# One memory ring for activations and token operands, the residual added later, weights first at the change of halves

## The chip, the core and the metric

The kernel runs on one core of one Trainium2 chip. The metric is the device time of one launch in microseconds (us). Three timed runs of the kernel before took 2837.26, 2839.12 and 2840.42 us. The core has engines that run side by side, each working through its own instructions in order: TensorE (PE) multiplies matrices, VectorE (DVE), ScalarE (ACT) and GpSimd (POOL) do elementwise work, SyncE (SP) issues DMAs. SBUF is the memory on the core, PSUM the eight banks into which PE accumulates. A tile is a piece of one of these memories. A ring is a set of equal tiles that are handed out in turn, and whoever wants one waits until the last user of it is done.

## The reference

One decoder layer on 2048 tokens of width 1024 in float32. What follows the attention, and matters here, is (`mix` is the gated sum of two attention branches):

```
x  = x + mix @ w_out                                   # out-projection, residual
h2 = rmsnorm(x, ln2_g)                                 # second norm
x  = x + square(relu(h2 @ w_up)) @ w_down              # w_up 1024 x 4096, w_down 4096 x 1024
```

## The kernel before

Every float32 product is made of three matmuls: each operand is split into a high part (a CAST on ACT) and a low part (a subtraction on POOL or DVE), `split` at L90, and `mm3` (L94) issues high x low, low x high and high x high (L96 to L98). A "128x512 matmul" below is one of the three.

The stages follow each other: in-projection and attention (to about 850 us of the span), gates and branches (to 1345), out-projection with the second norms (to 1553), up-projection (to about 2190), down-projection (2219 to 2833).

**Out-projection.** For each block of 128 tokens, PE multiplies, DVE adds the residual, and x goes out to `x2_dram`. `norm2_pre` (L776) squares the row on ACT into an own tile `junk`, POOL makes the scale (`ssy`, `rsxy` in `rms_scale`, L121), and DVE scales into `hn`. `norm2_post` (L783) transposes on PE and writes `hb`. For each pair of blocks POOL makes four differences (`hsum`, L809, names T1 to T4, a ring of three tiles), and each is stored to DRAM (`b_dram`).

**Up-projection.** The two matrix products of the MLP use the seven-product scheme of Strassen and Winograd, so the operands are sums: B11, T1, T2, B22, T3, B21, T4 of the tokens, and A11, S1, S2, S4, S3, A12, A22 of the weights. The tokens come in two halves (hf 0 and 1) of 1024. In each half `token_operand` (L831) loads and splits the seven token operands once, two loads of 512 KB each (`rb`), and 16 steps f follow. A step f loads two weight blocks (`rwu`, 512 KB each), `up_operands` (L848) makes its seven operands, and `up_products` (L919) runs seven products of 12 matmuls into three PSUM banks pa, pb, pc. ACT and DVE turn these into seven activation operands, which lie in one tile `u` of 7 x 512 (ring of two, plus three single tiles), and one DMA of 1792 KB stores them (L954). The weights of half 1, f = 0 are loaded after the last step of half 0 (the call of `up_operands` behind `up_products`, L1022).

**Down-projection.** Before it starts, the pools of the up-projection are released (L1028) and a pool `poolV` takes their place. `acc`, eight tiles that hold the result, is filled from `x2_dram` by 16 loads of 512 KB (L1037). Eight steps F follow, in each four groups g of tokens, in each seven products i. For each, `u_operand` (L1043) loads 256 KB of an activation operand (`ru`, on SP), splits it into `uo` (ACT, then POOL; a ring of nine), PE runs 24 matmuls into banks `pd`, and DVE adds them to `acc` (L1072). The weights (`rwd`) of the next F are loaded and split by `next_down_operands` (L998) after g = 1: seven operands wB11, wT1 and so on.

The raw loads of every stage share a ring `raw` of three tiles of 512 KB. All DMAs are issued by SP. A scheduler that simulates the program sets the order of the instructions on each engine. The order on chip is then fixed, and an instruction that waits holds up those behind it on its engine.

## Time and profile before

| | |
|---|---|
| median of three runs | 2839.12 us |
| profiled execution | 2838.56 us |
| its span (first to last instruction) | 2836.8 us |
| PE busy | 2729.4 us, 96% |
| POOL busy | 1581.9 us, 56% |
| DVE busy | 1510.3 us, 53% |
| ACT busy | 1285.9 us, 45% |
| DMA | 121 GB/s on average |

The profile is of one execution, whose time is 1.76 us longer than its span. PE is the engine to look at, because it is busy nearly throughout: time can only be won where it waits or runs slowly. PEclk in the views is the clock that was granted to TensorE, as a share of full speed, and DMA is the mean busy share of 16 DMA engines.

### The profile page before, as it was taken

What the parts mean: (1) busy time and instruction counts of PE and PEld (TensorE: products, weight loads), DVE (VectorE), ACT (ScalarE), POOL (GpSimd) and SP (SyncE); (2) the same over time, 40 slices, a digit from 0 to 9 for tenths busy, and PEclk for the clock granted to TensorE, in tenths of its full rate; (3) what the DMA queues carried; (4) which work ended last, traced back from release to release, by engine and by line L of the source; (5) the groups of instructions that cost most, each with busy time, mean ns of one, the idle gap of its engine ahead of it and who ended that gap; (6) DMA issues with size and microseconds to landing.
All of it is one profiled execution on the core that took longest, in us unless ns stands there. A gap on an engine that the chain in (4) does not pass through costs nothing.

```text
span 2836.8 us, 38641 instructions
## 1 busy us (share of the span) xinstructions
PE 2729.4 (96%) x13897; PEld 2280.2 (80%) x13897; DVE 1510.3 (53%) x2816; ACT 1285.9 (45%) x2607; POOL 1581.9 (56%) x1375
## 2 busy tenths in 40 slices
PE   8999999999979999999998999979999699999999
PEld 7888888887867888888787788868887588888887
DVE  7776665668995214111444443444344566666654
ACT  5565665667885213111222555555555333333331
POOL 6566666676671111111245766766675777777763
PEclk9999999999999999999999999999999899999999
DMA  5321010011234324222577455565546744444335
GB/s 170 98 71 52 11 57 12 15 57 37 58 102 151 93 68 152 84 63 68 194 225 230 153 155 163 163 186 164 157 151 204 260 128 127 125 123 121 106 108 175
DMA packets 372593, 342.83 MB, mean 121 GB/s; under 512 B 18080, under 2 KB 305840, under 8 KB 372400
## 3 DMA queue, kind: packets, MB, share of 16 engines
q1 hardware_dynamic: 372400, 340.36, 39.5%
q8 instruction: 109, 1.79, 0.3%
q14 instruction: 84, 0.69, 0.1%
HBM read 220.57 MB, written 119.73 MB: 120 GB/s over the span
## 4 chain that ended last, share of the span: by engine, by line
PE 85%; DMA 4%; POOL 4%; DVE 4%; issue 2%; ACT 1%; SPq 1%; POOLq 0%; DVEq 0%; ACTq 0%
PE pd L96 7%; PE pd L98 7%; PE pd L97 7%; PE pg L98 4%; PE pg L96 4%; PE pg L97 4%; PE psA L96 4%; PE psA L98 4%; PE psA L97 4%; PE pa L96 3%; PE pa L98 3%; PE pa L97 3%; PE pb L96 3%; PE pb L98 3%; PE pb L97 3%; PE sp L416 2%
## 5 line engine op out<-in xcount | busy, mean ns | idle before, releaser
L1072 DVE TENSOR_TENSOR acc<-acc,pd 128x512 f32<-128x512 f32 x448 | 298.3, 684 | 212.2 <-PE pd L98 212.1
L92 POOL TENSOR_TENSOR uo<-ru,uo 128x512 fp32r<-128x512 f32 x224 | 305.7, 1374 | 158.8 <-ACT uo L91 155.9
L91 ACT CAST uo<-ru 128x512 fp32r<-128x512 f32 x224 | 138.2, 621 | 344.8 <-PE pd L98 209.5
L96 PE MATMUL psA<-wah,hsh 128*128 128x512 f32 x512 | 208.6, 407 | 2.5 <-ACT hsh L91 1.0
L97 PE MATMUL psA<-wal,hsh 128*128 128x512 f32 x512 | 201.9, 394 | 5.2 <-DVE wal L92 5.2
L98 PE MATMUL psA<-wah,hsl 128*128 128x512 f32 x512 | 201.4, 393 | 1.2 <-DVE hsl L92 1.2
L97 PE MATMUL pd<-wT,uo 128*128 128x512 f32 x512 | 199.7, 390 | 0.0
L96 PE MATMUL pd<-wT,uo 128*128 128x512 f32 x512 | 198.4, 391 | 1.1 <-ACT wT L91 1.1
L98 PE MATMUL pd<-wT,uo 128*128 128x512 f32 x512 | 196.8, 389 | 0.0
L96 PE MATMUL pd<-wB,uo 128*128 128x512 f32 x384 | 150.2, 391 | 23.6 <-ACT uo L91 23.4
L97 PE MATMUL pd<-wB,uo 128*128 128x512 f32 x384 | 149.9, 390 | 0.0
L98 PE MATMUL pd<-wB,uo 128*128 128x512 f32 x384 | 148.7, 389 | 0.0
L653 DVE TENSOR_TENSOR sig<-sig,pb 128x512 f32<-128x512 f32 x64 | 43.7, 685 | 191.2 <-PE pb L98 169.5
L97 PE MATMUL psB<-wal,hsh 128*128 128x256 f32 x512 | 144.9, 283 | 0.0
L98 PE MATMUL psB<-wah,hsl 128*128 128x256 f32 x512 | 144.8, 283 | 0.0
L92 POOL TENSOR_TENSOR hsl<-hT,hsh 128x512 fp32r<-128x512 f32 x80 | 119.6, 1496 | 45.0 <-ACT hsh L91 40.6
L96 PE MATMUL psB<-wah,hsh 128*128 128x256 f32 x512 | 143.7, 281 | 0.0
L312 DVE TENSOR_REDUCE hss<-sq 128x8 f32<-128x512 f32 x64 | 43.8, 685 | 181.6 <-ACT sq L311 181.5
L318 POOL TENSOR_TENSOR hrs<-hss,mhalf 128x8 f32<-128x8 f32 (+1 forms) x64 | 137.2, 2143 | 5.2
L92 POOL TENSOR_TENSOR wg_1l<-rg,wg_1h 128x1024 fp32r<-128x1024 f32 x16 | 42.1, 2631 | 165.0 <-ACT wg_1h L91 130.6
L91 ACT CAST hsh<-hT 128x512 fp32r<-128x512 f32 x128 | 109.8, 858 | 47.3 <-PE psB L97 42.3
L345 POOL TENSOR_TENSOR qn<-qn,gains 128x512 f32<-128x512 f32 x48 | 69.8, 1455 | 81.0 <-DVE qn L342 72.9
(546 smaller groups left out, 8223.0 us busy)
## 6 DMA issues: line engine op xcount, KB each, us to landing
u_dram<-u SPq DMA_DIRECT2D x32, 1792.0 KB, 7.5
ru<-u_dram SPq DMA_DIRECT2D x224, 256.0 KB, 2.7
rwu<-in_w_up_dram SPq DMA_DIRECT2D x64, 512.0 KB, 3.8
x<-in_x_dram SPq DMA_DIRECT2D x32, 512.0 KB, 4.0
rg<-in_w_in_dram SPq DMA_DIRECT2D x32, 512.0 KB, 3.7
rwd<-in_w_down_dram SPq DMA_DIRECT2D x64, 256.0 KB, 3.1
rw<-in_w_in_dram SPq DMA_DIRECT2D x28, 384.0 KB, 3.4
hT_dram<-hT SPq DMA_DIRECT2D x16, 512.0 KB, 3.9
```

The costliest lines, as they stand in the source:

```text
L91: nc.scalar.copy(hi, src)
L92: (eng or nc.vector).tensor_tensor(lo, src, hi, op=ALU.subtract)
L96: nc.tensor.matmul(out, lhs[0], rhs[0], start=first, stop=False, skip_group_check=more)
L97: nc.tensor.matmul(out, lhs[0], rhs[1], start=False, stop=False, skip_group_check=more)
L98: nc.tensor.matmul(out, lhs[1], rhs[0], start=False, stop=last, skip_group_check=more)
L312: nc.vector.tensor_reduce(ss[:, 0:8], sq, axis=AX, op=ALU.add)
L318: nc.gpsimd.tensor_tensor(rs[:, 0:nh], ss[:, 0:nh], mhalf[:, 0:nh], op=ALU.pow)
L345: nc.gpsimd.tensor_tensor(q4, q4, gains[:, 0:2, :].unsqueeze(2).broadcast_to([P, 2, 4, HD]), op=ALU.mult)
L416: nc.tensor.matmul(sp[:, e * 256:e * 256 + nk], ring[:, own, q_, :], ring[:, slots, k_, :], start=(i == 0), stop=(i == 1))
L653: nc.vector.tensor_tensor(gate[m, c, a], gate[m, c, a], pb, op=ALU.mult)
L1072: nc.vector.tensor_tensor(t, t, p, op=ALU.add)
```

## The change

Seven edits: (1) The activations, the single tiles and the token operands of the down-projection share one ring of 18 tiles of 128x512 in `poolU`, which is no longer released between the stages. The store per step f becomes seven stores of 256 KB. (2) `u_load` loads two activation operands at a time (512 KB), and all but the first three of these 128 loads are issued by ACT. (3) `acc` is no longer loaded. In F = 0 the first product to touch each piece is copied by ACT, and the residual is loaded in 32 pieces of 256 KB during F = 1 and 2 and added by POOL. (4) `next_down_operands` is called after g = 2. (5) In the last step of half 0 the weight operands of half 1 are called for ahead of the products. (6) In the last step of half 1 the first three activation loads and four splits are called for ahead of the products. (7) In the out-projection `junk` is gone (the square goes into `hn`, now a ring of three), `hsum` is a ring of two, the low parts of the first four token operands are all made by DVE, and two sums of the weights of f = 0 (S4, S3) move from DVE to POOL.

```diff
-        junk = O4(f"junky{i}", "junk", 1, BF16)
-        rs = rms_scale(xt, junk, poolO, i, "y")
-        hn[i] = O4(f"hn{i}", "hn", 2, F32)
+        hn[i] = O4(f"hn{i}", "hn", 3, F32)
+        rs = rms_scale(xt, hn[i], poolO, i, "y")
...
-            t = poolO.tile([P, 4, P], F32, tag="hsum", bufs=3, name=f"hsum{n}_{i}")
+        return poolO.tile([P, 4, P], F32, tag="hsum", bufs=2, name=f"hsum{n}_{i}")
...
-            split(t[0][:, ks, :], t[1][:, ks, :], rv, nc.gpsimd if q else nc.vector)
+            split(t[0][:, ks, :], t[1][:, ks, :], rv, nc.gpsimd if q and (hf, o) > (0, 3) else nc.vector)
...
-        put("S4", summed("4", a12, s2, ALU.subtract, nc.vector))
-        put("S3", summed("3", a11, a21, ALU.subtract, nc.vector))
+        eng = nc.vector if f else nc.gpsimd
+        put("S4", summed("4", a12, s2, ALU.subtract, eng))
+        put("S3", summed("3", a11, a21, ALU.subtract, eng))
...
-    def Ft(name):
-        return poolF.tile([P, 512], F32, tag="f", bufs=3, name=name)
+    def Ft(name, dtype=F32):
+        return poolU.tile([P, 512], dtype, tag="u", bufs=18, name=name)
...
-        nc.sync.dma_start(u_ops_dram[hf][f // 2][:, :, :, f % 2, :], u.rearrange("p o (j t) -> p o j t", j=4))
+        for o in (6, 1, 0, 2, 4, 5, 3):
+            nc.sync.dma_start(u_ops_dram[hf][f // 2][:, o, :, f % 2, :], u[o].rearrange("p (j t) -> p j t", j=4))
...
+    def u_load(F, g, o):
+        hf, j = g // 2, 2 * (g % 2)
+        no = min(2, 7 - o)
+        r = raw(f"ru{F}_{g}_{o}").rearrange("p (o n) -> p o n", o=2)
+        queue = nc.sync if (F, g) == (0, 0) and o < 6 else nc.scalar
+        queue.dma_start(r[:, 0:no].rearrange("p o (j f t) -> p o j f t", j=2, f=2),
+                        u_ops_dram[hf][F][:, o:o + no, j:j + 2, :, :])
...
+        t = [Ft(f"uo{e}{F}_{g}_{o}", F32R) for e in "hl"]
+        split(t[0], t[1], u_raw.pop((F, g, o)), nc.gpsimd)
...
+            if last and hf == 0:
+                A_next = up_operands(1, 0)
+            if last and hf == 1:
+                for o in (0, 2, 4):
+                    u_load(0, 0, o)
+                U_first = [u_operand(0, 0, o) for o in range(4)]
             up_products(hf, f, A, Bops[hf], then)
-            if f + 1 < NF or hf == 0:
-                A_next = up_operands(hf + last, 0 if last else f + 1)
+            if not last:
+                A_next = up_operands(hf, f + 1)
...
-    poolF.release()
-    poolU.release()
-    poolV = tc.alloc_tile_pool(name="mV", bufs=1, reuse_waits="tile")
...
-            nc.sync.dma_start(a[:, c, :], x2_dram[i * P:(i + 1) * P, :])
...
+    def add_residual(p, c, n):
+        ns = slice(n * 512, (n + 1) * 512)
+        r = poolS.tile([P, 512], F32, tag="S", bufs=12, name=f"rx2_{p}_{c}_{n}")
+        nc.sync.dma_start(r, x2_dram[acc_block(p, c), ns])
+        nc.gpsimd.tensor_tensor(acc[p][:, c, ns], acc[p][:, c, ns], r, op=ALU.add)
...
-                U = u_operand(F, g, i)
+                U = U_first.pop(0) if U_first else u_operand(F, g, i)
+                if 1 <= F <= 2 and i in (3, 6):
+                    for n in range(2):
+                        add_residual(2 * ((g + 3) % 4) + i // 6, (F - 1) % 2, n)
...
-                    nc.vector.tensor_tensor(t, t, p, op=ALU.add)
+                    if F == 0 and i in (0, 1, 2, 6):
+                        nc.scalar.copy(t, p)
+                    else:
+                        nc.vector.tensor_tensor(t, t, p, op=ALU.add)
...
-            if g == 1 and F + 1 < NFF:
+            if g == 2 and F + 1 < NFF:
                 next_down_operands(F + 1, B_NAMES)
```

SP's queue at the change of halves, before. `rwu0_15` are the weights of half 0, step 15, `rb1_T2` to `rb1_T4` token operands of half 1, `rwu1_0` the first weights of half 1, `u_0_13` to `u_0_15` the activations of the last steps:

```order
L853 DMA rwu0_15_1_17671<-in_w_up_dram 128x4x256
L841 DMA rb1_T2_0_17729<-b_dram1_T2_13820 128x1024
L954 DMA u2_dram0_6_15429<-u_0_13_17403 3584x1x128
L841 DMA rb1_T2_1_17733<-b_dram1_T2_13820 128x1024
L841 DMA rb1_B22_0_17752<-b_dram1_B22_13821 128x1024
...
L841 DMA rb1_T4_1_17830<-b_dram1_T4_13824 128x1024
L853 DMA rwu1_0_0_17867<-in_w_up_dram 128x4x256
L853 DMA rwu1_0_1_17869<-in_w_up_dram 128x4x256
```

And the same place with the change:

```order
L859 DMA rwu0_15_1_17832<-in_w_up_dram 128x4x256
L859 DMA rwu1_0_0_17870<-in_w_up_dram 128x4x256
...
L967 DMA u2_dram0_7_15411<-u0_0_14_17710 128x4x128
L859 DMA rwu1_0_1_17872<-in_w_up_dram 128x4x256
L847 DMA rb1_T2_0_17931<-b_dram1_T2_13820 128x1024
...
L847 DMA rb1_B21_1_18006<-b_dram1_B21_13823 128x1024
L967 DMA u2_dram0_7_15411<-u6_0_15_17911 128x4x128
...
L847 DMA rb1_T4_1_18033<-b_dram1_T4_13824 128x1024
```

The two weight loads of half 1 stood behind all ten loads of token operands and now stand ahead of them.

SP's queue between the up- and the down-projection, before. `acc` is the result with the residual, `rwd0` and `rwd1` are down-projection weights of F = 0 and 1, `ru0_0` activation operands of F = 0, g = 0:

```order
L1047 DMA ru0_0_2_20385<-u2_dram0_0_15423 128x512
L954 DMA u2_dram1_7_15438<-u_1_14_20013 3584x1x128
L1037 DMA acc0_20274<-x2_dram_13810 128x1024 x2
L1037 DMA acc1_20277<-x2_dram_13810 128x1024 x2
L1004 DMA rwd0_0_1_0_20313<-in_w_down_dram 128x512
...
L1004 DMA rwd0_1_1_1_20323<-in_w_down_dram 128x512
L954 DMA u2_dram1_7_15438<-u_1_15_20161 3584x1x128
...
L1004 DMA rwd1_1_1_1_20633<-in_w_down_dram 128x512
L1047 DMA ru0_0_3_20404<-u2_dram0_0_15423 128x512
```

And with the change (`u0_1_13` and so on are single stores of 256 KB, `rx2` a piece of the residual):

```order
L967 DMA u2_dram1_6_15418<-u4_1_13_20288 128x4x128
L1031 DMA ru0_0_0_20514<-u2_dram0_0_15404 128x2x512
...
L1031 DMA ru0_0_4_20518<-u2_dram0_0_15404 128x2x512
L967 DMA u2_dram1_7_15419<-u4_1_14_20448 128x4x128
L1017 DMA rwd0_0_0_0_20670<-in_w_down_dram 128x512
...
L1017 DMA rwd1_1_1_1_21119<-in_w_down_dram 128x512
L1080 DMA rx2_6_0_0_21376<-x2_dram_13810 128x512
L967 DMA u2_dram1_7_15419<-u2_1_15_20628 128x4x128
```

The 16 loads of `acc` are gone, and the first three activation loads stand ahead of all down-projection weights.

ACT's order around the last up-projection step (half 1, f = 15), before. `pa1_15` is its last PSUM bank, `uo0_0_0` the first activation operand of the down-projection:

```order
L925 ACTIVATE u_1_15_20161<-pa1_15_20163 128x512
L926 ACTIVATE u_1_15_20161<-u_1_15_20161 128x512
L91 CAST wT3_0_20333<-wT3s0_0_20331 128x512
...
L91 CAST wT4_0_20346<-wT1s0_1_20327 128x512
L91 CAST uo0_0_0_20306<-ru0_0_0_20304 128x512
L91 CAST uo0_0_1_20368<-ru0_0_1_20366 128x512
```

And with the change (`acc0` to `acc1` are the copies of F = 0):

```order
L91 CAST uoh0_0_2_20528<-ru0_0_2_20516 128x512
L91 CAST uoh0_0_3_20532<-ru0_0_2_20516 128x512
L945 COPY u0_1_15_20536<-pa1_15_20539 128x512
L947 COPY u6_1_15_20537<-pb1_15_20540 128x512
L1031 DMA ru0_0_6_20805<-u2_dram0_0_15404 128x512
L1112 COPY acc0_20656<-pd0_0_0_0_20664 128x512
...
L937 ACTIVATE u5_1_15_20644<-pa1_15_20539 128x512
L91 CAST wT4_0_20707<-wT1s0_1_20688 128x512
L91 CAST wB11_1_21121<-rwd1_1_0_0_21113 128x512
L938 ACTIVATE u5_1_15_20644<-u5_1_15_20644 128x512
L91 CAST uoh0_0_4_20769<-ru0_0_4_20518 128x512
```

The first four activation operands are now cast ahead of the first copy of step f = 15, the fifth (`uoh0_0_4`) behind its last activation.

## Rows read from the trace of the kernel before

**Rows 1.** Page, busy time: us, share of the span, instructions.
```profile
PE 2729.4 (96%) x13897; PEld 2280.2 (80%) x13897; DVE 1510.3 (53%) x2816; ACT 1285.9 (45%) x2607; POOL 1581.9 (56%) x1375
```

**Rows 2.** Stretches, PE alone: start:end length, PE busy (matmuls), PEclk, DMA, GB/s.
```profile
1562.00:1592.00 30.00, 23.79 (x86) 0.89 0.61 192
1602.00:1850.00 248.00, 248.00 (x1096) 1.00 0.54 161
1850.00:1900.00 50.00, 33.71 (x133) 0.86 0.66 206
1880.00:1890.00 10.00, 4.33 (x9) 0.50 0.93 285
2190.00:2250.00 60.00, 34.78 (x139) 0.80 0.88 312
2200.00:2210.00 10.00, 0.00 (x0) 0.50 1.04 421
2250.00:2820.00 570.00, 570.00 (x2516) 1.00 0.45 127
```

**Rows 3.** Waits of PE, whole span: waited for, us in total, times, longest us.
```profile
PE pd L96 <- ACT uo L91: 23.4, 1, 23.4
PE pa L96 <- ACT A11h L91: 12.4, 1, 12.4
PE h2ps L796 <- DVE hn L781: 8.1, 3, 3.7
PE pa L96 <- ACT T4h L91: 2.4, 1, 2.4
```

**Rows 4.** Chain of waits, change of halves: start us, us, what.
```profile
1870.84 6.02 DMA rb_B<-b_dram_B
1876.89 1.05 ACT B21h L91
1880.39 4.40 DMA rwu<-in_w_up_dram
1885.56 1.29 POOL A11l L92
```

**Rows 5.** Chain of waits, between up- and down-projection.
```profile
2190.98 7.87 DMA acc<-x_dram
2198.87 8.17 DMA rwd<-in_w_down_dram
2207.05 8.77 DMA rwd<-in_w_down_dram
2219.16 1.28 POOL wT L92
```

**Rows 6.** Chain of waits, start of the up-projection.
```profile
1560.00 3.46 DMA b_dram_T<-hsumT
1563.58 0.60 DVE T3l L92
```

**Rows 7.** Groups by shape, ACT, 1552 to 2219: busy us, mean ns | idle before.
```profile
L926 ACT ACTIVATE u<-u 128x512 f32<-128x512 f32 x96 | 60.6, 633 | 2.3
L933 ACT COPY u<-pa 128x512 f32<-128x512 f32 x32 | 18.5, 579 | 0.5 <-PE pa L98 0.5
L91 ACT CAST B21h<-rb_B 128x1024 fp32r<-128x1024 f32 x4 | 4.2, 1046 | 4.9 <-DMA rb_B<-b_dram_B 4.9
```

**Rows 8.** Groups by shape, POOL, 1610 to 2190.
```profile
L859 POOL TENSOR_TENSOR s<-s,rwu 128x512 f32<-128x512 f32 x28 | 42.4, 1515 | 1.9
L92 POOL TENSOR_TENSOR S4l<-s,S4h 128x512 fp32r<-128x512 f32 x29 | 37.6, 1297 | 49.1 <-ACT S4h L91 49.1
L92 POOL TENSOR_TENSOR S3l<-s,S3h 128x512 fp32r<-128x512 f32 x29 | 45.7, 1577 | 5.2 <-ACT S3h L91 5.2
```

**Rows 9.** Groups by shape, 2219 to 2834 (down-projection).
```profile
L92 POOL TENSOR_TENSOR uo<-ru,uo 128x512 fp32r<-128x512 f32 x224 | 305.7, 1374 | 158.8 <-ACT uo L91 155.9 <-DMA ru<-u_dram 2.2
L1072 DVE TENSOR_TENSOR acc<-acc,pd 128x512 f32<-128x512 f32 x448 | 298.3, 684 | 212.2 <-PE pd L98 212.1
```

**Rows 10.** Stretches, all engines: PE, PEld, DVE, ACT, POOL busy, PEclk, DMA, GB/s.
```profile
1350.00:1552.00 202.00, 191.32 (x893) 158.10 (x891) 94.06 (x102) 46.96 (x63) 82.45 (x73) 0.99 0.70 220
2370.00:2446.00 76.00, 76.00 (x337) 62.93 (x336) 48.05 (x65) 24.68 (x43) 56.99 (x43) 1.00 0.45 125
```

**Rows 11.** SP's queue, 2183 us: start us, us, instruction (a DMA's issue).
```profile
2182.22 0.33 SPq L1047 DMA_DIRECT2D ru<-u_dram  x1
2183.38 0.53 SPq L954 DMA_DIRECT2D u_dram<-u  x1
```

More of the change, by code (lines that the diff above doesn't have):

```diff
@@ L102, in hybrid_layer @@
     make_identity(nc, ident)
-    mhalf = const.tile([P, 10], F32, name="mhalf")
+    mhalf = const.tile([P, 12], F32, name="mhalf")
     nc.vector.memset(mhalf, -0.5)
@@ L797, in norm2_post @@
             ks = slice(4 * half, 4 * half + 4)
-            t2 = hb[half, c] = poolO.tile([P, 4, P], F32, tag="hb", bufs=6, name=f"hb{i}_{half}")
+            t2 = hb[half, c] = tile_hb(i, half)
             nc.vector.tensor_tensor(t2, pt.rearrange("p (j t) -> p j t", j=4),
@@ L816, in norm2_post, with hb_tile, hsum_tile @@
         summed("T4", hb[1, 0], t2)
+    def hb_tile(i, half):
+        return poolO.tile([P, 4, P], F32, tag="hb", bufs=6, name=f"hb{i}_{half}")
+    def hsum_tile(n, i):
+        return poolO.tile([P, 4, P], F32, tag="hsum", bufs=2, name=f"hsum{n}_{i}")
     def load_mix(i):
@@ L896, in hybrid_layer @@
         if n > 0:
-            norm2_post(order[n - 1])
+            norm2_post(order[n - 1], hb_tile, hsum_tile)
         norm2_pre(i)
@@ L902, in hybrid_layer @@
     A_next = up_operands(0, 0)
-    norm2_post(order[-1])
+    norm2_post(order[-1], hb_tile, hsum_tile)
     poolO.release()
@@ L910, in hybrid_layer, with new @@
     poolU = tc.alloc_tile_pool(name="mU", bufs=1, reuse_waits="tile")
[L911 removed]
     u_ops_dram = [[dram.tile([P, 7, 4, 2, P], F32, name=f"u2_dram{hf}_{F}") for F in range(NF // 2)] for hf in range(2)]
[L916 to L917 removed]
+    def Ft(name, dtype=F32):
+        return poolU.tile([P, 512], dtype, tag="u", bufs=18, name=name)
     def up_products(hf, f, A, B, then):
[L920 to L921 removed]
+        u = {}
+        def new(o):
+            u[o] = Ft(f"u{o}_{hf}_{f}")
+            return u[o]
+        a11, a22, a21 = new(0), new(6), Ft(f"a21_{hf}_{f}")
         ps = [bank(f"p{n}{hf}_{f}") for n in "abc"]
@@ L943, in up_products @@
                 relu2(a22)
-                nc.vector.tensor_tensor(u[:, 1, :], a21, a22, op=ALU.add)
+                nc.vector.tensor_tensor(new(1), a21, a22, op=ALU.add)
             elif i == 5:
@@ L1007, in next_down_operands, with u_operand @@
                                               bufs=12 if n == "T1" else 2, name=f"w{n}s{F}_{f}"))
+    u_raw = {}
+    def u_load(F, g, o):
[5 more added lines that the diff above has]
+                        u_ops_dram[hf][F][:, o:o + no, j:j + 2, :, :])
+        for e in range(no):
+            u_raw[F, g, o + e] = r[:, e, :]
+    def u_operand(F, g, o):
+        if (F, g, o) not in u_raw:
+            u_load(F, g, o)
+        t = [Ft(f"uo{e}{F}_{g}_{o}", F32R) for e in "hl"]
+        split(t[0], t[1], u_raw.pop((F, g, o)), nc.gpsimd)
+        return [t_.rearrange("p (j f t) -> p j f t", j=2, f=2) for t_ in t]
+    U_first = []
     for hf in range(2):
@@ L1027, in hybrid_layer, with acc_block @@
                 first_down_operands()
-    poolF.release()
-    poolU.release()
-    poolV = tc.alloc_tile_pool(name="mV", bufs=1, reuse_waits="tile")
-    acc = []
-    for p in range(8):
-        a = poolT1.tile([P, 2, D], F32, tag="t", bufs=8, name=f"acc{p}")
-        for c in range(2):
-            i = 8 * (p // 4) + 4 * c + p % 4
-            nc.sync.dma_start(a[:, c, :], x2_dram[i * P:(i + 1) * P, :])
-        acc.append(a)
+    acc = [poolT1.tile([P, 2, D], F32, tag="t", bufs=8, name=f"acc{p}") for p in range(8)]
+    def acc_block(p, c):
+        i = 8 * (p // 4) + 4 * c + p % 4
+        return slice(i * P, (i + 1) * P)
+    def add_residual(p, c, n):
[3 more added lines that the diff above has]
+        nc.gpsimd.tensor_tensor(acc[p][:, c, ns], acc[p][:, c, ns], r, op=ALU.add)
     GOES = ((0, 0), (1, 1), (0, 1), (0, 1), (1, 1), (0, 0), (1, 0))
     LAST = {3: (0, 1), 4: (1, 1), 5: (0, 0), 6: (1, 0)}
-    def u_operand(F, g, o):
-        hf, j = g // 2, 2 * (g % 2)
-        r = raw(f"ru{F}_{g}_{o}")[:, 0:512]
-        nc.sync.dma_start(r.rearrange("p (j f t) -> p j f t", j=2, f=2), u_ops_dram[hf][F][:, o, j:j + 2, :, :])
-        t = poolV.tile([P, 2, 512], F32R, tag="v", bufs=9, name=f"uo{F}_{g}_{o}")
-        split(t[:, 0, :], t[:, 1, :], r, nc.gpsimd)
-        return t.rearrange("p h (j f t) -> p h j f t", j=2, f=2)
     NFF = NF // 2
@@ L1064, in hybrid_layer @@
                     for f in range(2):
-                        mm3(p, [U[:, e, q, f, :] for e in range(2)], [w[:, e, f, :] for e in range(2)],
+                        mm3(p, [U[e][:, q, f, :] for e in range(2)], [w[:, e, f, :] for e in range(2)],
                             f == 0 and first, f == 1, not first)
@@ L1071, in hybrid_layer @@
                     t = acc[2 * g + q][:, c, ns]
-                    nc.vector.tensor_tensor(t, t, p, op=ALU.add)
+                    if F == 0 and i in (0, 1, 2, 6):
+                        nc.scalar.copy(t, p)
+                    else:
+                        nc.vector.tensor_tensor(t, t, p, op=ALU.add)
                     if F == NFF - 1 and i in LAST:
-                        pr = 2 * g + q
-                        b = 8 * (pr // 4) + 4 * c + pr % 4
-                        nc.sync.dma_start(out[b * P:(b + 1) * P, ns], t)
-            if g == 1 and F + 1 < NFF:
+                        nc.sync.dma_start(out[acc_block(2 * g + q, c), ns], t)
+            if g == 2 and F + 1 < NFF:
                 next_down_operands(F + 1, B_NAMES)
-    for pool in (poolV, pools["T2"], poolS, poolT1, edge, dram, psp, rawp, const):
+    for pool in (poolU, pools["T2"], poolS, poolT1, edge, dram, psp, rawp, const):
         pool.release()
```

21 lines of the change are left out of this document (10 added, 11 removed).

## The prediction

> **What bounds the kernel now.** I read the busy times first: PE works 2729.4 of 2836.8 us [rows 1], so what can be won is where PE stands still or is slow. Next I read the stretches of PE. At full pace it ends one 128x512 matmul every 0.2266 us: 570.00 us for 2516 in the down-projection, and 248.00 us for 1096 in the up-projection, with no gap in either [rows 2]. That rate turns any other stretch into a loss: matmuls that would fit, less those that ran, times 0.2266. Three stretches that the change touches fall short [rows 2]:
>
> - start of the up-projection, 1562 to 1592: 132.4 would fit, 86 ran, loss 10.5 us;
> - change of halves, 1850 to 1900: 220.7 against 133, loss 19.9 us;
> - up to down, 2190 to 2250: 264.8 against 139, loss 28.5 us.
>
> Then the waits. At the change of halves PE waits 12.4 us for one operand, A11h; between up and down it waits 23.4 us for one `uo` [rows 3]. The loss is larger than the wait, because around the long waits the granted clock reads 0.50 (of the two levels 1.2 and 2.4 GHz, the lower) and the matmuls after it are slow [rows 2]. The chain tells what is late. At the change of halves the last token operands come first and the weights of the new half stand behind them: 6.02 us of `rb`, a cast of 1.05, then 4.40 us of `rwu` and 1.29 us for A11's low part [rows 4]. Between up and down it is DMA alone, one load of `acc` and two of `rwd` of about 8 us each [rows 5], at a DMA share of 1.04 and 421 GB/s [rows 2]. The DMA engines are fully busy there: 16 loads of 512 KB for `acc` lie in front of the weights in SP's queue.
>
> **Change of halves (edit 5).** The weights now stand ahead of the ten token loads, and PE's order runs the first two products of the new half inside the last products of the old one, so the 12.4 us wait goes. Next late is ACT. After the last product of the old half it must do a relu and a square, two casts of token operands and a copy before PE has what it needs: 2 x 0.633 + 2 x 1.046 + 0.579 [rows 7] = 3.9 us. At the start of the up-projection single waits such as the 2.4 us for T4h [rows 3] went along with a clock of 0.89 [rows 2], so I add 2 us. I take 6 us left of 19.9, a saving of 13.9. Bounds: nothing left (saving 19.9), or the ten token loads, whose bytes are the same, stay late by themselves and all is left (saving 0).
>
> **Up to down (edits 1, 3, 6).** 8 MB of `acc` loads leave the queue, and the pools are no longer exchanged there. The 23.4 us wait, whose chain is `acc` and `rwd`, loses both of its causes. Next late is the fifth activation operand. The first four are cast ahead of step 15, so that PE has four products of 12 matmuls (2.72 us each) to run. The cast of the fifth stands behind the relu of the last product, two casts of weights and the square: 2 x 0.633 for relu and square, and three casts at half of B21h's 1.046 for twice the size, together 2.8 us [rows 7]. Behind it POOL has, per operand, the low part and two low parts of weights, 3 x 1.374 = 4.1 us [rows 9] against the 2.72 of a product, for about three operands: 3 x 1.4 = 4.2 us. Sum 7 us, a saving of 21.5. Bounds: all gone (28.5), or half of it left, if weights that now start earlier only meet the stores of the last steps (14).
>
> **Residual on POOL (edit 3).** In F = 1 POOL's program holds 57 operations instead of 42, in F = 2 it holds 56. One F takes PE 76 us [rows 10]. At 1.374 us for the 41 or 40 splits [rows 9] and 1.515 us for the 16 additions, the price of the nearest POOL operation with two plain inputs in the trace [rows 8], that is 56.3 + 24.2 = 80.5 us, and 79.2 in the second, so POOL falls behind by 4.5 + 3.2 = 7.7 us. The cover is the ring of nine split operands, seven beyond the two in use: 7 x 2.72 = 19 us. I take nothing. Bounds: nothing, or, if every POOL operation took the 1.577 us of the slowest group [rows 8], 89.9 and 88.3 us, 26 us behind, 7 us beyond the cover.
> GpSimd's operations do differ by what runs beside them: the same shape takes 1297 ns as S4l and 1577 ns as S3l [rows 8]. The Trainium skill ("GPSIMD Engine Reference", section "Specifications") says that its way into SBUF is shared with VectorE and that VectorE's operations with two SBUF inputs contend for it, which speaks against this edit. The two rows agree with it as far as they go; by the rule at its worst the sum would be 7 us higher.
>
> **First touch on ACT (edit 3).** 32 DVE additions of 0.684 us [rows 9] become 32 copies of about 0.579 [rows 7]. ACT is busy 24.7 us of 76 there [rows 10], so in themselves they cost nothing. A copy must be done before PE comes back to its bank, one product (2.72 us) later; that cover holds while ACT isn't held up.
>
> **Loads on ACT's queue (edit 2).** 224 loads of 256 KB become 128, 125 of them on ACT. The trace shows no issue on ACT; on SP an issue takes 0.33 to 0.53 us [rows 11], so 16 in an F are 5 to 8 us of an engine that is idle for 51. I take nothing; the upper bound is in the rivals. The store of 1792 KB becomes seven of 256 KB on SP: 7 x 0.53 = 3.7 us of SP per step of 19 us (84 matmuls), hidden, with the same bytes. Moving the weights' loads to g = 2 (edit 4) leaves them a g (19 us) and the ring of operands ahead, and their chain of load, cast and low part is hidden today; nothing.
>
> **Out-projection (edit 7).** With two tiles for `hsum`, T3 waits until the store of T1 has landed and T4 for that of T3, about 3.46 us each [rows 6]. POOL is busy 82 of 202 us there [rows 10], so for most pairs this is slack. PE's waits for `hn` (8.1 us) [rows 3] may move either way, as the scale now stands ahead of T3. At the last pair nothing hides it: today the up-projection's T3l starts when the last store has landed [rows 6], and now the last store goes out one landing later, 3.5 us. Four token splits and two sums change engine around it; S4 and S3 on POOL add 2 x 1.5 [rows 8], on a path that is only partly exposed. I take 4 us more loss at the start of the up-projection. Bounds: 2 us less (DVE relieves POOL), 9 us more (the waits repeat with the clock, as the 10.5 us there show).
>
> **Sum.** -13.9 - 21.5 + 4 = -31.4 us. The profiled execution took 2838.56 us (its span and 1.76 outside it), within 0.6 us of the median, so I forecast 2807 us. The bounds of the terms all at their best give -19.9 - 28.5 - 2 = 2788, all at their worst without a rival 0 - 14 + 7 + 9 = 2841.
>
> **Rivals.**
>
> *Full cover (chance 0.13).* The scheduler placed casts and loads so that ACT's 3.9 and 2.8 us stand beside matmuls of the other half. For it: PE's new order has filler products in both places. Against it: ACT's order has the operand's cast behind the last relu in both. Losses of 2 us each place and none at the start: -17.9 - 26.5 = 2794.
>
> *One boundary only (0.16).* At the change of halves the ten token loads and now seven small stores per step share SP's queue and three raw tiles, so the wait moves from A11h to a token operand. For it: the 6.02 us load in the chain and a DMA share of 0.93 [rows 2, 4]. Against it: the last two token loads stand well behind the products that run first. Saving there 3 instead of 13.9: -3 - 21.5 + 4 = 2818.
>
> *ACT's queue (slower, 0.13).* A load on ACT waits until POOL has freed a raw tile, and every cast and copy behind it waits with it. In F = 1 and 2 POOL has no time to spare, so each time that ACT's wait lets POOL run dry is lost for good. 32 loads stand there. Two us lost at each make 64; with the 7.7 us that POOL is behind and 19 of cover, 53 us reach PE, and the time is 2807 + 53 = 2860. It decides from (31.4 + 19 - 7.7) / 32 = 1.3 us per load. For it: a 512 KB load takes 4.40 us [rows 4], longer than the 2.72 of a product. Against it: three raw tiles hold six operands, 16 us of PE, and POOL's wait for `uo` is mostly slack today [rows 9].
> The Trainium skill ("Perfetto Trace Analysis", section "DMA Instruction — HWDGE (DVE, Sync)") describes a sequencer that issues a DMA as held first by its semaphores and then by a lock on the descriptor generator that it shares with the other issuing engine. That is this rival's mechanism with ACT and SP as the two; no row here shows an issue on ACT.
>
> *No net change (0.08).* The gains are given back in pieces: half of each boundary (-9.9 - 14.2), with 9 lost at the start and 13 in F = 1 and 2, is -2, and gives about 2836.
>
> **How the numbers follow.** The forecast (2798 to 2816 by its own bounds) has 0.50. Faster by over 0.2%, which is about what a measurement here can tell from no change, holds the forecast, full cover and one boundary: 0.50 + 0.13 + 0.16 = 0.79; same 0.08; slower 0.13. The range from 2795 to 2837 leaves out the slower rival and the lower half of full cover.
>
> **What would show it.** Right: the waits for A11h and `uo` gone from PE's waits, short ones for T2h, B21l or uoh in their place; the two stretches short of matmuls by some 25 to 30 each; DMA share below 1 between up and down; POOL near full in F = 1 and 2 and PE without gaps. Wrong: PE waiting for uol in F = 1 to 3, ACT idle behind its own loads, or a loss at the start of the up-projection that has doubled.

## The result and the profile after

The change made the kernel slower: 2856.73 us (median of 4 runs, 2855.65 to 2857.58) against 2838.57 us for the kernel before beside it. The ratio is 1.0062, with a 95% interval of 1.005 to 1.0075. The profiled span grew from 2836.8 to 2855.3 us, by 18.5. The ratios here and below leave out two runs far off all others, one of e18 (7034 us) and one of the kernel before beside e16 and e17 (3343 us).

The stretches of PE, after (columns as in [rows 2]):

```profile
1850.00:1900.00 50.00, 45.12 (x186) 0.97 0.57 163
1900.00:1950.00 50.00, 39.38 (x159) 0.90 0.63 192
2190.00:2250.00 60.00, 52.69 (x228) 0.95 0.67 207
2240.00:2250.00 10.00, 2.69 (x7) 0.72 0.87 278
2320.00:2400.00 80.00, 80.00 (x354) 1.00 0.59 179
2400.00:2480.00 80.00, 79.97 (x352) 1.00 0.55 166
```

Between up and down 228 matmuls run instead of 139, and the DMA share is 0.67 instead of 0.88 [rows 2]; the stretch is the same in time, not in work, as the changed kernel gets there later. At the change of halves the loss has not gone, it has spread: 7.9 us in the first stretch and 14.0 in the second, by 0.2266 us for each missing matmul. In F = 1 and 2 (the last two rows) PE has no gap.

PE's waits, 1300 to 2840, after (columns as in [rows 3]):

```profile
PE h2ps L796 <- DVE hn L781: 11.4, 3, 5.0
PE pc L96 <- ACT B21h L91: 8.3, 1, 8.3
PE pc L98 <- POOL A12l L92: 7.8, 5, 3.5
PE pd L96 <- ACT uoh L91: 7.3, 2, 4.1
PE pa L96 <- ACT u L945: 5.4, 2, 3.6
PE pa L97 <- DVE T3l L92: 3.5, 1, 3.5
```

The waits for `uo` (23.4) and A11h (12.4) [rows 3] are gone. In their place stand a token operand (B21h, 8.3), a weight's low part (A12l), a copy of the last steps (`u`) and, at the start of the up-projection, a low part of a token operand (T3l).

The first copy out of bank pa in a step marks the same work in every kernel. The regions are cut at set distances from three of these copies: the first step's (from 3 us before it to 100 behind it), that of the first step of half 1 (85 before, 65 behind) and the last step's (80 before, 10 behind). The loss (time less 0.2266 us per matmul) by region, us, of one execution each; "steady" is the steps between:

| | out-proj. | start of up | change of halves | last steps | up to down, down | steady |
|---|---|---|---|---|---|---|
| before | -1.3 | 10.5 | 19.9 | 0.7 | 28.7 | -0.8 |
| after | 6.0 | 14.8 | 27.4 | 10.7 | 12.7 | 3.7 |
| e2 | -1.3 | 11.9 | 23.1 | 7.3 | 13.0 | 4.3 |
| e3 | 2.2 | 11.7 | 20.6 | 6.1 | 13.0 | 4.2 |
| e4 | 2.0 | 13.0 | 27.2 | 6.1 | 12.9 | 3.6 |
| e8 | 3.0 | 11.2 | 19.5 | 6.6 | 12.4 | 2.8 |
| e10 | -0.2 | 12.3 | 24.4 | 10.9 | 24.8 | 3.9 |
| e16 | -0.7 | 11.4 | 24.0 | 9.3 | 11.2 | 4.1 |
| e17 | -0.8 | 12.6 | 20.6 | 7.3 | 12.6 | 3.0 |

(The out-projection also runs shorter matmuls, so only its differences count.) From before to after: +7.3, +4.3, +7.5, +10.0, -16.0 and +4.5, together +17.6 of the 18.5 us.

### The profile page after: what moved, and what is told of

Its sections match the earlier page's. It is cut to its first block, busy times and chain, and to the rows that moved or that the text cites. A ratio compares the mean times of both kernels' runs of the same rounds, so it can differ in the third digit from the quotient of the medians.

```text
span 2855.3 us, 38962 instructions
## 1 busy us (share of the span) xinstructions
PE 2746.8 (96%) x13897; PEld 2287.9 (80%) x13897; DVE 1470.8 (52%) x2784; ACT 1301.0 (46%) x2639; POOL 1604.6 (56%) x1407
## 5 line engine op out<-in xcount | busy, mean ns | idle before, releaser
L1114 DVE TENSOR_TENSOR acc<-acc,pd 128x512 f32<-128x512 f32 x416 | 275.4, 683 | 220.0 <-PE pd L98 207.1
L92 POOL TENSOR_TENSOR uol<-ru,uoh 128x512 fp32r<-128x512 f32 x224 | 302.6, 1368 | 117.4 <-ACT uoh L91 87.1
L91 ACT CAST uoh<-ru 128x512 fp32r<-128x512 f32 x224 | 137.6, 622 | 311.6 <-PE pd L97 226.6
L96 PE MATMUL pd<-wT,uoh 128*128 128x512 f32 x512 | 199.5, 392 | 5.2 <-ACT uoh L91 4.1
L97 PE MATMUL pd<-wT,uoh 128*128 128x512 f32 x512 | 200.2, 391 | 0.0
L98 PE MATMUL pd<-wT,uol 128*128 128x512 f32 x512 | 198.3, 391 | 0.0
L96 PE MATMUL pd<-wB,uoh 128*128 128x512 f32 x384 | 149.4, 391 | 3.2 <-ACT uoh L91 3.2
L97 PE MATMUL pd<-wB,uoh 128*128 128x512 f32 x384 | 149.9, 390 | 0.0
L98 PE MATMUL pd<-wB,uol 128*128 128x512 f32 x384 | 148.2, 389 | 0.0
L96 PEld LDWEIGHTS pd<-wT,uoh 128*128 128x128 f32 x512 | 96.5, 189 | 26.8 <-ACT uoh L91 4.5
```

Of the source, the lines that this page charges most:

```text
L91: nc.scalar.copy(hi, src)
L92: (eng or nc.vector).tensor_tensor(lo, src, hi, op=ALU.subtract)
L96: nc.tensor.matmul(out, lhs[0], rhs[0], start=first, stop=False, skip_group_check=more)
L97: nc.tensor.matmul(out, lhs[0], rhs[1], start=False, stop=False, skip_group_check=more)
L98: nc.tensor.matmul(out, lhs[1], rhs[0], start=False, stop=last, skip_group_check=more)
L1114: nc.vector.tensor_tensor(t, t, p, op=ALU.add)
```

## The experiments

Each was timed beside the kernel before (medians of 2838.8 to 2840.3 us). Diffs are against the changed kernel unless another is named.

**e1. The kernel before, with seven stores per step.**
```
-        nc.sync.dma_start(u_ops_dram[...], u.rearrange(...))
+        for o in (6, 1, 0, 2, 4, 5, 3):
+            nc.sync.dma_start(u_ops_dram[hf][f // 2][:, o, ...], u[:, o, :]...)
```


> The kernel before, with its one store of 1792 KB per step f cut into seven of 256 KB on SP, and nothing else. Theory A (SP works in order, so each small store that waits for its activation holds up the weight and token loads behind it; this is why the changed kernel waits for A12l, S1l and A11l in the steps with token loads): 6 to 20 us slower than the kernel before, 2845 to 2859, with new waits of PE for A12l or S1l between 1810 and 1960 us. Theory B (the stores cost only SP time that is hidden; the waits come from the order in which weights and tokens are called for): within 2 us of the kernel before, 2837 to 2841.


Measured 2841.76 us, ratio 1.0009 (1.0 to 1.0019), with the regions within 2.1 us of before. The stores by themselves are worth about 3 us in the kernel before, not 18. In the changed kernel, where weight loads stand behind them, they were not tried apart.

**e2. Edit 7 undone.**
```
-        hn[i] = O4(f"hn{i}", "hn", 3, F32)
+        junk = O4(f"junky{i}", "junk", 1, BF16)
...
-        return poolO.tile([P, 4, P], F32, tag="hsum", bufs=2, ...)
+        return poolO.tile([P, 4, P], F32, tag="hsum", bufs=3, ...)
...
```


> The changed kernel with the out-projection of before (edit 7 undone: own tile for the square, three tiles for hsum, low parts of the first token operands on POOL, S4 and S3 of f = 0 on DVE). Theory C (edit 7 costs the 8.3 us by which the first step of the up-projection is late and the further 13.4 us up to its fifth step): 15 to 22 us faster than the changed kernel, 2835 to 2842, with waits for hn back at 8 us. Rival (the start of the up-projection is late because of the small stores and the shared ring, not of edit 7): 0 to 8 us faster, 2849 to 2857.


Measured 2840.71 us, 1.0015 (0.9998 to 1.0033): 16 us back. Three of its ten runs lie at 2852 to 2857 (see e18).

**e3. Only hsum a ring of three again.**
```
-        return poolO.tile([P, 4, P], F32, tag="hsum", bufs=2, ...)
+        return poolO.tile([P, 4, P], F32, tag="hsum", bufs=3, ...)
```


> The changed kernel with three tiles for hsum instead of two, the rest of edit 7 kept. If the ring of two alone makes the out-projection and the start of the up-projection late (T3 waits for the store of T1, T4 for that of T3): within 4 us of the kernel with the whole old out-projection. If the splits moved to DVE or the sums moved to POOL do it: within 4 us of the changed kernel, 2853 to 2857.


Measured 2842.95 us, 1.0017 (1.0002 to 1.0032): one number is worth 13.8 us. What the ring of two does is seen in the changed kernel. POOL waits 41.1 us for stores of `hsum` to land, in eleven waits; with the ring of three the trace shows no such wait. POOL's waits from 1350 to 1600, and then one of them in the timelines of POOL, SP and ACT (start, us, instruction, then idle time before it and what ended it):

```profile
POOL hsumT L809 <- DMA b_dram_T<-hsumT: 41.1, 11, 7.3
```
```profile
1508.84 1.30 POOL L809 TENSOR_TENSOR hsumT<-hb,hsumT 128x512 f32<-128x512 f32 x1 [5.47 <-DMA b_dram_T<-hsumT]
```
```profile
1510.16 0.51 SPq L790 DMA_DIRECT2D b_dram_T<-hsumT  x1
1510.77 0.58 SPq L847 DMA_DIRECT2D rb_B<-b_dram_B  x1
```
```profile
1516.16 1.05 ACT L91 CAST B22h<-rb_B 128x1024 fp32r<-128x1024 f32 x1 [6.15 <-DMA rb_B<-b_dram_B]
```

POOL stands until a store of `hsum` has landed, SP stands until POOL has made the next difference, and a token load goes out behind that store, at 1510.77. In e3 it goes out at 1505.74, and the cast waits 2.74 us instead of 6.15. Little of this reaches PE at once. Its waits for `hn` are 11.4 us against 9.7 in e3, and the longest, 4.98, is 4.68 there. At the start of the up-projection it waits 3.5 us for T3l (0.7 in e3, and 3.5 again in e4, which has the ring of two).

Out-projection and start give back only 3.8 + 3.1 us; 6.8 come back at the change of halves and 4.6 in the last steps. Apart from the first steps, PE's orders of the two programs differ in just these two places, some 300 and 600 us behind the edit: the scheduler, which simulates the program, arranged them otherwise.

**e4. Edit 5 undone: the weights behind the last step.**
```
-            if last and hf == 0:
-                A_next = up_operands(1, 0)
...
-            if not last:
-                A_next = up_operands(hf, f + 1)
+            if f + 1 < NF or hf == 0:
+                A_next = up_operands(hf + last, 0 if last else f + 1)
```


> The changed kernel with edit 5 undone: the weights of half 1, f = 0 are called for after the last products of half 0. Theory D (weights first removes a wait of 12 us for A11h, and other waits have come beside it): 8 to 16 us slower than the changed kernel, 2865 to 2873, with the wait for A11h back. Rival (weights first only moves the wait to the token operands, B21h 8.3 us, at no gain): within 3 us of the changed kernel, 2854 to 2860.


Measured 2849.36 us, 1.0038 (1.0024 to 1.0052). The wait for A11h is back (6.3 us), yet the loss at the change of halves is 27.2, as with the weights first. So neither theory holds: it is 7 us faster, and the regions that gained are the out-projection (loss 2.0 instead of 6.0) and the last steps (6.1 instead of 10.7), which edit 5 does not touch.

**e5. e3, with the token operands of half 1 loaded in quarters into the 12 tiles "S" instead of the raw ring.**
```
+        for q in range(4 if hf else 0):
+            r = poolS.tile([P, 512], F32, tag="S", bufs=12, ...)
+            nc.sync.dma_start(r, b_dram[hf][n][:, q, :])
...
```


> The kernel with three hsum tiles, and the token operands of half 1 loaded in quarters of 256 KB into the 12 tiles of 128x512 that otherwise hold down-projection weights and lie idle then, instead of into the ring raw of three. Theory R (at the change of halves weights and tokens share the three raw tiles; weights first hold two of them until their last low part is made, so B21 and T4 are loaded too late and PE waits 8.2 us for B21h): 8 to 14 us faster than the kernel with three hsum tiles (2843 us), 2829 to 2835, the wait for B21h under 3 us. Rival (the casts on ACT and the freeing of the old half's tiles set the time, whatever the loads do): within 3 us of it, 2840 to 2846.


Measured 2863.26 us, 1.0083 (1.0068 to 1.0098): a miss, 20 us slower than e3, with 41.9 us lost at the change of halves. SP there:

```profile
1882.30 9.83 SPq L863 DMA_DIRECT2D rwu<-in_w_up_dram  x2
1892.22 1.01 SPq L971 DMA_DIRECT2D u_dram<-u  x2
1893.54 1.13 SPq L845 DMA_DIRECT2D rb_T<-b_dram_T  x2
```

SP stands 9.83 us at weight loads, and the first load of T2 goes out behind them. The tiles are not idle, though the expectation calls them so: `up_operands` keeps the weight operands of every step in this ring, 14 tiles a step in a ring of 12. So e5 does not take the token loads out of a shared ring, it puts them into another; the same holds for what e6 to e9, e11, e12 and e17 load there.

**e6. e5, with the first down-projection weights loaded apart as well.**
```
-                r.append(raw(f"rwd0_{f}_{m}"))
+                    r[m, n] = poolS.tile([P, 512], F32, tag="S", bufs=12, ...)
...
```


> The kernel before this one in the list, and the first down-projection weights (loaded during step 11 of half 1) also in those tiles instead of raw. Theory R for the last steps of half 1 (ACT stands at the cast of a weight whose load waited for a raw tile, and PE at its copy behind it, 3.6 us, with a slow clock after it, 6.3 us lost): 4 to 7 us faster than the kernel with only the tokens apart. Rival (the loads come late because SP stands at the small stores): no change, within 2 us.


Measured 2867.53 us, 1.0103 (1.0087 to 1.0119): worse again, with 16.1 us in the last steps.

**e7. e6 with edit 5 undone (as in e4).**


> The same with the weights of half 1, f = 0 called for after the last products again (edit 5 undone). If weights first is worth what the prediction said once the raw tiles are no longer shared: 6 to 14 us slower than the kernel before this one in the list, with a wait for A11h back. If the order is worth nothing: within 2 us of it.


Measured 2855.95 us, 1.0058 (1.0033 to 1.0082); the change of halves falls from 40.3 to 26.9 us. Weights in front of the tokens cost 13 us there, where both wait for the same tiles.

**e8. e3, with the loads of T2 and B22 of half 1 called two steps earlier.**
```
+            if hf == 0 and f == NF - 3:
+                for o in (2, 3):
+                    token_load(1, o)
...
```


> The kernel with three hsum tiles, and the loads of two token operands of half 1 (T2, B22) called for two steps earlier, into the idle tiles of 128x512 (quarters of 256 KB); in SP's queue they then stand between the two weight loads of half 1 instead of behind both, and the other three keep to raw. Theory S (SP works in order and stands at a weight load that waits for a raw tile, and the token loads behind it come late, in the changed kernel as in the run with the tokens in other tiles, where SP stood 9.8 us at weight loads): 8 to 14 us faster than the kernel with three hsum tiles (2843 us), 2829 to 2835, the stretch around the change of halves short by 7 to 12 us instead of 20.6. Rival (the work itself is too much there: casts on ACT and low parts on POOL and DVE of five token operands beside the weights' operands): the stretch stays short by 18 to 24 us, 2840 to 2846.


Measured 2839.9 us, 1.0006 (0.9989 to 1.0022). The 8.2 us wait for B21h is gone, but 19.5 us are still lost, in waits of 3 us and less: theory S holds in part only.

**e9. e8 with edit 5 undone.**


> The same with the weights of half 1, f = 0 called for after the last products (edit 5 undone). Theory S: token loads then stand ahead of all weights and are in time, the weights come late: a wait for A11h of 4 to 12 us, within 4 us of the kernel with two early tokens, or slower. If weights first costs in itself, as the changed kernel suggests (7.4 us faster without it): 5 to 9 us faster than the kernel with two early tokens.


Measured 2840.21 us, 1.0015 (0.9998 to 1.0032), with A11h at 7.5 us: as S says.

**e10. e3 with edit 5 undone.**


> The changed kernel with three hsum tiles and edit 5 undone, and nothing else. If the two effects add (13.8 and 7.4 us): 2834 to 2838. If the 7.4 us of undoing edit 5 were only the shift of other instructions that comes with any new order: 2840 to 2846.


Measured 2857.12 us, 1.0059 (1.0042 to 1.0075), where every theory had less: a new stand in F = 2. DVE, then POOL, then PE:

```profile
2452.48 14.03 DVE L988 TENSOR_TENSOR wT3s<-rwd,rwd 128x512 f32<-128x512 f32 x1 [2.96 <-POOL wT L92]
2466.44 0.67 DVE L1112 TENSOR_TENSOR acc<-acc,pd 128x512 f32<-128x512 f32 x1
2467.03 0.68 DVE L988 TENSOR_TENSOR wT3s<-rwd,rwd 128x512 f32<-128x512 f32 x1
```
```profile
2451.16 2.54 POOL L92 TENSOR_TENSOR wT<-wT3s,wT 128x512 fp32r<-128x512 f32 x2
2453.66 1.29 POOL L92 TENSOR_TENSOR uol<-ru,uoh 128x512 fp32r<-128x512 f32 x1
2454.92 2.51 POOL L92 TENSOR_TENSOR wB<-rwd,wB 128x512 fp32r<-128x512 f32 x2
2457.39 1.26 POOL L92 TENSOR_TENSOR uol<-ru,uoh 128x512 fp32r<-128x512 f32 x1
2458.61 2.48 POOL L92 TENSOR_TENSOR wT<-wT1s,wT 128x512 fp32r<-128x512 f32 x2
2461.05 1.26 POOL L92 TENSOR_TENSOR uol<-ru,uoh 128x512 fp32r<-128x512 f32 x1
2462.27 2.48 POOL L92 TENSOR_TENSOR wB<-rwd,wB 128x512 fp32r<-128x512 f32 x2
2464.71 1.26 POOL L92 TENSOR_TENSOR uol<-ru,uoh 128x512 fp32r<-128x512 f32 x1
2470.30 2.83 POOL L92 TENSOR_TENSOR wT<-wT1s,wT 128x512 fp32r<-128x512 f32 x2 [4.33 <-ACT wT L91]
```
```profile
2468.37 0.80 PE L96 MATMUL pd<-wT,uoh 128*128 128x512 f32 x1 [11.63 <-DVE acc L1112]
```

One subtraction on DVE with both inputs in SBUF takes 14.03 us; the same one takes 0.68 a moment later. POOL works without a break all that time, and DVE ends 0.5 us after POOL's last operation (2464.71 + 1.26). The additions to `acc` stand behind it on DVE, and PE waits for them.

**e11. e5, with these token loads from the third operand on issued by ACT.**
```
-            nc.sync.dma_start(r, b_dram[hf][n][:, q, :])
+            (nc.scalar if o >= 2 else nc.sync).dma_start(r, b_dram[hf][n][:, q, :])
```


> As e5_tokens_apart (2863.3 us, loss at the change of halves 41.9 us), but the quarter loads of the last five token operands of half 1 are issued by ACT instead of SP, so that no weight load that waits for a raw tile stands in front of them. Theory Q (in e5 the token loads were late because SP stood at weight loads in front of them): the 9.8 us stand of SP no longer reaches PE, the loss at the change of halves falls by at least 15 us, and the time to 2840 to 2850 us. Theory V (what is late there is the work behind the loads, casts and low parts, or DMA bandwidth): the loss stays above 35 us and the time at 2858 to 2870.


Measured 2868.62 us, 1.0097 (1.0069 to 1.0124), 45.1 us lost: theory Q fell. ACT, off SP's queue, issues T2's first load no earlier. That load, PE's last matmul of half 0 in e11, and the same matmul in e5:

```profile
1898.50 1.06 ACTq L845 DMA_DIRECT2D rb_T<-b_dram_T  x2
```
```profile
1898.30 0.39 PE L98 MATMUL pa<-T4h,A22l 128*128 128x512 f32 x1
```
```profile
1893.34 0.39 PE L98 MATMUL pa<-T4h,A22l 128*128 128x512 f32 x1
```

So SP's stand in e5 was not the cause. In both kernels the load goes out 0.2 us after PE has started the last matmul on A22l (1893.54 against 1893.34 in e5), and A22l lies in the ring that the load wants a tile of. The likely cause is thus that the weight operands, called for ahead, hold these tiles; no edit tried it apart.

**e12. e2 with e8's two early loads.**


> The changed kernel with edit 7 undone (as e2_old_outproj, 2840.7 us) and with the loads of T2 and B22 called two steps earlier (as in e8_two_tokens_early, which against the ring of three alone gained 3 us in time). Theory A (the two are worth what they were alone): 2836 to 2839 us, at or just under the kernel before. Theory O (each edit draws another order over the whole program, and what one of them gives is lost elsewhere): outside 2834 to 2841, in either direction, and the regions that neither edit touches (last steps of half 1, up to down) differ from e2's 7.3 and 13.0 us by over 3 us.


Measured 2837.01 us, 0.9996 (0.9981 to 1.0011); nine runs at 2833.99 to 2840.67, one at 2854.36.

**e13. e3 without ten token loads of half 1 (half 1's output is not the layer's).**
```
...
+            split(h, l, ident.unsqueeze(1).broadcast_to([P, 8, P]), ...)
...
```


> The ring of three (e3_hsum3, 2843 us, loss at the change of halves 20.6 us) with the loads of the last five token operands of half 1 left out: they are cast and subtracted from a constant in SBUF instead, so the casts and low parts are all there, and the output of half 1 is not that of the layer. Theory L (what is late at the change of halves is these ten loads, by SP's order, the raw ring and the DMA engines): the loss falls to 8 us or less, and the time by 12 to 2829 to 2833 us. Theory W (it is ACT's and POOL's work of splitting seven token operands and seven weight operands within the few products before they are needed): the loss stays at 15 us or more, the time at 2838 to 2845.


Measured 2833.55 us, 0.9988 (0.9973 to 1.0003). 17.9 us are still lost at the change of halves, 2.7 less than in e3: by the region theory W, though the time fell by 9, of which the trace shows 3.3 in the out-projection. PE's waits there, 1820 to 1960:

```profile
PE pc L98 <- POOL A12l L92: 5.7, 3, 2.9
PE pa L98 <- POOL A11l L92: 3.6, 2, 1.9
```

Without these loads PE waits for POOL's low parts of the weights. POOL (the fifth busy time in the row, behind PE, PEld, DVE and ACT) is busy for 39.92 of the 40 us from 1860 to 1900:

```profile
1860.00:1900.00 40.00, 34.76 (x142) 27.20 (x141) 26.29 (x19) 26.04 (x42) 39.92 (x23) 0.96 0.47 134
```

**e14. e3 with edit 6 undone.**
```
-            if last and hf == 1:
-                for o in (0, 2, 4):
-                    u_load(0, 0, o)
-                U_first = [u_operand(0, 0, o) for o in range(4)]
```


> The ring of three (e3_hsum3) with edit 6 undone: the first activation loads and splits are no longer called for ahead of the last step's products. Theory H (the calls ahead cost the last steps of half 1 what they save after them): the loss in the last steps falls from 6.1 to 2 or less and that from there on rises from 13.0 by as much, time within 3 us of 2843. Theory P (edit 6 is worth what I put on it): up to down loses 10 us or more on top, 2851 to 2858. Theory I (neither: the last steps lose by wB casts that wait for loads behind seven stores on SP): the last steps still lose 5 us or more.


Measured 2844.33 us, 1.0024 (1.0013 to 1.0034), with 8.9 us lost in the last steps (e3: 6.1): edit 6 is worth little, and it is not why they lose time. The profiled run, like e13's, has the 14 us stand of e10.

**e15. e3 with the first down-projection weights called a step earlier.**
```
-            if hf == 1 and f == NF - 5:
+            if hf == 1 and f == NF - 6:
```


> The ring of three (e3_hsum3) with the first down-projection weights called for one step earlier. Theory I (the last steps of half 1 lose 6 us because casts of wB wait on ACT for loads that stand behind the stores): the loss there falls to 2 us or less, time 2837 to 2840. Theory N (the lateness is made elsewhere): the loss stays within 2 us of 6.1, time within 3 us of 2843.


Measured 2844.78 us, 1.003 (1.0015 to 1.0046); 8.0 us in the last steps: theory N. The steady steps lose 4 us more than in e3.

**e16. e10 with the residual added on DVE. e17. e12 likewise. e18. e3 likewise.**
```
-        nc.gpsimd.tensor_tensor(acc[p][:, c, ns], acc[p][:, c, ns], r, op=ALU.add)
+        nc.vector.tensor_tensor(acc[p][:, c, ns], acc[p][:, c, ns], r, op=ALU.add)
```


> The kernel of e10_hsum3_weights_last (2857.1 us, all runs 2856.6 to 2858.0, PE waits 11.6 us for DVE at 2457) with the 32 residual additions on DVE instead of POOL; no order before F = 1 changes. Theory G (POOL, kept busy without a break by the residual additions, holds up the DVE subtraction wT3s, which took 14.03 us instead of 0.68 and ended as soon as POOL paused; PE waited for the additions behind it): no DVE operation over 3 us in F = 1 to 3, no PE wait for acc over 2 us, and the time falls by 10 to 13 us to 2844 to 2847. Theory K (the stand of DVE has another cause, such as late loads of rwd or a wait that the profile does not show): the 14 us operation stays and the time stays at 2853 or more.

> The kernel of e12_old_outproj_tokens_early (2837.0 us; nine runs 2834.0 to 2840.7, one 2854.4) with the residual additions on DVE. Theory G: the run that lay 14 to 20 us above the rest no longer occurs (spread under 9 us), the median is 2834 to 2837 us, at or 0.1 to 0.2% under the kernel before. Theory K: runs 12 us or more above the median still occur, about one in ten, or the additions on DVE cost PE time and the median is 2839 or more.

> The changed kernel with two lines of it taken back: hsum a ring of three (as e3_hsum3, 2843.0 us, seven runs 2836.2 to 2843.6 and three 2848.3 to 2854.5) and the residual added on DVE. Theory G: the upper group of runs goes, all lie within 9 us, the median is 2837 to 2841 us; with the two lines the change comes out even with the kernel before, its gain of 16 us between up and down spent at the start, the change of halves, the last steps and in the steady steps. Theory K: the upper group stays and the median is 2842 or more.


e16: 2843.62 us, 13.5 less than e10. Its groups on DVE, 2300 to 2560, and those of e10 before it (busy us, mean ns | idle before):

```profile
L988 DVE TENSOR_TENSOR wT3s<-rwd,rwd 128x512 f32<-128x512 f32 x8 | 26.4, 3297 | 11.6 <-DMA rwd<-in_w_down_dram 8.6 <-POOL wT L92 3.0
```
```profile
L1079 DVE TENSOR_TENSOR acc<-acc,rx 128x512 f32<-128x512 f32 x29 | 32.4, 1118 | 0.6
L988 DVE TENSOR_TENSOR wT3s<-rwd,rwd 128x512 f32<-128x512 f32 x8 | 9.1, 1139 | 5.5 <-DMA rwd<-in_w_down_dram 5.1 <-POOL wT L92 0.4
```

(The first fence is e10, the second e16.) The long wait is gone. e17: 2836.52 us, 0.9992 (0.9983 to 1.0001), all 11 runs within 6.6 us. e18: 2839.14 us, 0.9998 (0.9989 to 1.0007); its eleven other runs lie at 2835.97 to 2841.21, where e3 had three of ten at 2848 to 2855. So that upper group was most likely DVE's stand: no trace of it was taken in e3, but e13's and e14's traces are of such upper runs and show the stand. Theory G holds in all three. Against e3's seven lower runs (median 2840.2) the ring of two costs 16.5 us. No version is clearly faster than the kernel before.

## Why the prediction was wrong

The forecast was 2807 us, and the time is 2856.7. Of the 49.0 us between the forecast (-31.4) and the regions' sum (+17.6), 21.4 lie at the change of halves, 10.0 in the last steps, 7.3 in the out-projection, 5.5 between up and down, 4.5 in the steady steps and 0.3 at the start.

**Up to down, -21.5: right in mechanism, too large.** The wait for `uo` went, and `uoh` is next, 7.3 us. Of 28.7 us 12.7 are left instead of 7: the clock falls there again, 0.72 at 2240 to 2250. The saving is 16.0. None of PE's waits there is for POOL's low parts, on which the prediction had put 4.2 us.

**Start of the up-projection, +4: right** (10.5 to 14.8), and in mechanism: PE waits 3.5 us for T3l (0.5 before), as the last store goes out later.

**Out-projection, nothing in the sum: +7.3.** "For most pairs this is slack" read POOL's 82 of 202 us [rows 10] as freedom to wait. But POOL, SP and ACT work in order, and behind POOL's wait stood a store, a load and a cast (e3). An engine's idle share says nothing of who is queued behind a wait. I bounded the term of edit 7 at 9 us; the ring alone is worth 14 to 16.5 (e3, e18). Of e3's 13.8 about 7 fall in the out-projection and the start, and the rest where the scheduler made another order, which the prediction did not consider at all. How much of the 7.3 is POOL's wait is not settled: e4, with the same out-projection, loses only 2.0 there, and the eighteen traces with a ring of three lie between -1.7 and 3.0.

**Change of halves, -13.9: the step that failed most, +7.5.** The A11h wait went as forecast, but the loss that came with it did not. I took ACT's 3.9 us as what is next late and 6 us as what is left; 27.4 are left. In the place of A11h came B21h. SP's queue, then what SP waits for from 1845 to 1912, then ACT:

```profile
1851.60 7.61 SPq L859 DMA_DIRECT2D rwu<-in_w_up_dram  x2
...
1878.65 0.33 SPq L847 DMA_DIRECT2D rb_T<-b_dram_T  x1
...
1902.58 1.40 SPq L847 DMA_DIRECT2D rb_B<-b_dram_B  x2
```
```profile
SPq L847 <- POOL A22l L92: 10.6, 2, 9.7
```
```profile
1908.97 1.04 ACT L91 CAST B21h<-rb_B 128x1024 fp32r<-128x1024 f32 x1 [2.20 <-DMA rb_B<-b_dram_B]
```

SP stands 7.61 us at weights, and the first token load behind them waits 9.7 us more, until POOL's low part of A22 has freed a raw tile. That is the mechanism of the rival "one boundary only", which still had a saving of 3. But it isn't all: taking this wait away (e8), moving the weights back (e4, e9) or leaving the token loads out (e13) leaves 18 to 27 us each time. Five token and seven weight operands are split there, and in e13 POOL's low parts are what PE waits for. That POOL, which has no pause there in e13, is the floor is a reading of that trace, not shown by an edit on POOL. In the changed kernel itself POOL is busy for 27.58 of the 40 us from 1860 to 1900.

**Last steps of half 1, not in the sum: +10.0.** In the changed kernel SP stands 9.39 us at two loads of `rwd`, so the second goes out at about 2146.5, and ACT waits 4.68 us for it with the copy behind that PE needs:

```profile
2137.44 9.39 SPq L1007 DMA_DIRECT2D rwd<-in_w_down_dram  x2
2146.92 7.37 SPq L967 DMA_DIRECT2D u_dram<-u  x6
```
```profile
2151.39 0.62 ACT L91 CAST wB<-rwd 128x512 fp32r<-128x512 f32 x1 [4.68 <-DMA rwd<-in_w_down_dram]
...
2153.08 0.57 ACT L945 COPY u<-pa 128x512 f32<-128x512 f32 x1
```

The prediction had no term for the loads that now wait for raw tiles here. e3, with another order, loses 4.6 us less in the same place, and e15 moved the loads and won nothing, so what sets this loss stays open, as does the +4.5 us of the steady steps.

**Residual on POOL, 0: right in this kernel, by luck of the order.** F = 1 and 2 run without gaps. But I priced POOL's backlog, 7.7 us against a cover of 19, and not what a full POOL does to DVE. e10 and e16 show that price, 11.6 us of PE in one stand. I had weighed the rule for it: the Trainium skill ("GPSIMD Engine Reference", section "Specifications") has POOL share its way into SBUF with VectorE, whose operations with two SBUF inputs contend for it. Another page of the Trainium skill ("SBUF — State Buffer", section "Summary: rules for kernel authors") says that in this case the second to issue fully blocks until the first finishes. The trace agrees with the blocking, but DVE stood through eleven POOL operations in a row (the second `wT` at 2452.4 to the `uol` that ends at 2465.97), not one. I had made the rule a charge of 7 us on POOL; it struck the other engine.

**ACT's queue and the copies, 0: right.** ACT issued 125 loads, and PE has no gap in F = 1 and 2.

## What to carry to other kernels

Before a ring is made smaller, follow what is queued behind the first wait that this adds, on every engine that issues in order; an idle share of 60% did not show that it was covered. Where a scheduler sets the order, time each edit of a bundle alone: here one ring's size changed the order 300 and 600 us further on, and that cost more (11.4 us) than the ring did on the spot (6.9). Leave POOL gaps wherever DVE has operations with two SBUF inputs ahead of PE's: here 32 operations moved from POOL to DVE ended the long stands. And before idle tiles are borrowed, read the kernel for who else uses their ring (e5).
